# A decoder block on one core: float32 matmuls of attention and state space grouped into pairs and quarters, with four small edits beside it

## The chip, the core and the metric

The kernel runs on one core of a Trainium2 chip. A core has a matrix engine (TensorE, in the views PE, with PEld for its weight loads), a vector engine (VectorE, DVE), a scalar engine (ScalarE, ACT), a general engine (GpSimd, POOL) and a queue engine (SyncE, SP) that starts transfers. Each engine takes its instructions strictly in the order of the program; they meet at semaphores. The metric is the device time of one execution in microseconds (us), the median of the runs.

## The reference

One decoder layer on 256 tokens of width 1024. A normalised input is projected into q, k, v, u and a gate. Attention over eight heads and a state-space branch over u run side by side, are mixed by sigmoid gates, projected and added to the input; a squared-ReLU MLP and a last normalisation follow. All is float32.

```python
h = rms_norm(x, norm_mix_g)
q, k, v, u, g = split(h @ w_in)
q, k = rotary(q, pos), rotary(k, pos)
o_a = softmax(mask(q @ k.T * HEAD_DIM ** -0.5)) @ v          # 8 heads of 128, one block of 256 keys
# state space: a complex diagonal recurrence over 256 tokens, 32 groups of 64 states
xr0, xi0 = (cr + 1j * ci) * (u @ b)                          # per group
sr, si = scan(a, xr0, xi0)
y = sr @ c_re.T - si @ c_im.T + d_skip * u
val, gt = split(gelu(y) @ w_glu)
o_b = val * sigmoid(gt)
mixed = sigmoid(g_a) * o_a + sigmoid(g_b) * o_b
x = x + mixed @ w_out
x = x + square(relu(rms_norm(x, norm_mlp_g) @ w_up)) @ w_down
return rms_norm(x, norm_final_g)
```

## The kernel before

**Two kinds of matmul.** The large products (projections, GLU, output, MLP) split each float32 operand into a high and a low part and add three products of parts (`mm3`, `tok_mm`, `down`). ScalarE makes a weight tile's high part (`hi_`, line 83) and VectorE its low part (`lo_`, line 84), four tiles of each in turn, so a `hi_` cast waits until TensorE has left the tile four before it. The small products run on whole float32 operands, and each such instruction shows as two matmul records, a transpose as one: the scores `s` (`attn_head`, with two bf16 products that add the mask), the transposes `pt` of the probabilities and the outputs `o` (`attn_out`), the inputs `x` and outputs `y` of the state space (`ssm_quad`), the transposes `bt` of its input matrices (`prepare`), and `mt`, the transposes of the gated branch. `x` uses 64 rows of the array and `y` against `sr` and `si` 64 columns, so two of them run at a time; the others use the whole array.

**Attention** goes by four pairs of heads, S0 to S3 for scores and softmax, A0 to A3 for transposes, outputs and the multiply into `mixA`. The softmax of a head: two maxima on VectorE (`st`), two exponentials on ScalarE into `pr`, reciprocals on VectorE, two scalings of `pr` on ScalarE (lines 323, 324); then three transposes on TensorE, a copy `pts` on ScalarE, four matmuls.

**The state space** goes by four quads of state tiles: `tables(m)` makes cosines and sines of the phases (a high part by ScalarE, line 516, a low part by four VectorE instructions, line 520), `ssm_quad(m)` multiplies, scans and multiplies back. `prepare` builds the input matrices `Bs`, which GpSimd puts in place from `ab` (line 455).

**The order** of the work is written out by hand, in `ORDER`; Vn are the parts of v, Pn and Cn the preparation, Tn the tables, Kn the q and k of a pair, Gn its gate, Qn a quad, Bn the other gate, Xn the loads of ScalarE's function tables and Yn the gelu:

```python
ORDER = ("V0 V1 P0 T0 C0 Q0 T1 Q1 T2 K0 T3 X0 S0 G0 A0 G1 K1 K2 S1 Q2 A1 K3 G2 S2 A2 Q3 "
         "B0 G3 S3 X1 Y0 A3 B1")
```

A scheduler then lays each engine's instructions by due times of its own, with a lead for those under `high_priority` (the scores and outputs have `ATT_PRIO`), so the small matmuls come to lie within streams of large ones. `use_set` loads a table of functions (1.28 us) and holds each table's functions together: the exponentials of S3 must come before X1, and the gelus behind it.

Of the kernel before, what the change touches and what calls it, by code (L numbers as in the profile page):

```python
# [16 lines left out]
P = 128  # L17
# [31 lines left out]
def build(ctx, tc, dr, out):  # L49
# [45 lines left out]
    def behind(ins, others, reason="table set"):  # L95
        for o in others:
            tc.add_manual_dep(ins, o.name, mybir.DependencyInfo(
                mybir.DependencyClass.NoSync, mybir.DependencyReason.DATA), reason=reason)

    def use_set(func):  # L100
# [132 lines left out]
    for c in range(2):  # L233
        V.tensor_mul(u[:, 2 * c : 2 * c + 2], by_parity(u_acc[:, c]), rs_par)
    V.tensor_mul(rcos, cos_c, rs)
    V.tensor_mul(rsin, sin_c, rs)
    for q in range(4):
# [63 lines left out]

    scale = P ** -0.5
    mixA = p1.tile([P, KD, T], F32, name="mixA")

    def attn_head(q, k, j):
        s = att_bank("s").rearrange("p a b -> p (a b)")
        PE.matmul(s[:, 0:128], q[:, j, 0:128], k[:, j, 0:128], start=True, stop=False,
                  skip_group_check=True)
        PE.matmul(s[:, 0:128], ident_b, tri_b, start=False, stop=True, skip_group_check=True)
        PE.matmul(s[:, 128:384], q[:, j, 128:256], k[:, j, :], start=True, stop=False,  # L310
                  skip_group_check=True)
        PE.matmul(s[:, 256:384], ident_b, tri_b, start=False, stop=True, skip_group_check=True)
        st = p1.tile([P, 6], F32, tag="st", bufs=2, name="st")
        V.tensor_reduce(st[:, 0:1], s[:, 0:128], axis=mybir.AxisListType.X, op=ALU.max)
        V.tensor_reduce(st[:, 1:2], s[:, 128:384], axis=mybir.AxisListType.X, op=ALU.max)
        V.tensor_scalar(st[:, 0:2], st[:, 0:2], -scale, None, op0=ALU.mult)
        pr = p1.tile([P, 384], F32, tag="pr", bufs=2, name="pr")
        act(pr[:, 0:128], s[:, 0:128], AF.Exp, bias=st[:, 0:1], scale=scale,
                     accum_out=st[:, 2:3])
        act(pr[:, 128:384], s[:, 128:384], AF.Exp, bias=st[:, 1:2], scale=scale,  # L320
                     accum_out=st[:, 3:4])
        V.reciprocal(st[:, 4:6], st[:, 2:4])
        S.activation(pr[:, 0:128], pr[:, 0:128], AF.Copy, scale=st[:, 4:5])
        S.activation(pr[:, 128:384], pr[:, 128:384], AF.Copy, scale=st[:, 5:6])
        return pr

    def attn_pt(pr):
        pt = att_bank("pt").rearrange("p a b -> p (a b)")
        for i in range(3):
            PE.transpose(pt[:, i * P : (i + 1) * P], pr[:, i * P : (i + 1) * P], ident)  # L330
        pts = p1.tile([P, 384], F32, tag="pts", bufs=2, name="pts")
        S.copy(pts, pt[:, 0:384])
        return pts

    def attn_out(hp, prs, tha):
        pts = [attn_pt(x) for x in prs]
        o = att_bank("o")
        for j in range(2):
            hd = 2 * hp + j
            PE.matmul(o[:, j, :], v[:, 0, hd * P : (hd + 1) * P], pts[j][:, 0:256],  # L340
                      start=True, stop=False, skip_group_check=True)
            PE.matmul(o[:, j, 128:256], v[:, 1, hd * P : (hd + 1) * P], pts[j][:, 256:384],
                      start=False, stop=True, skip_group_check=True)
        V.scalar_tensor_tensor(mixA[:, 2 * hp : 2 * hp + 2, :], tha, 1.0, o,
                               op0=ALU.add, op1=ALU.mult)

# [12 lines left out]
    def prepare():  # L359
# [91 lines left out]

        def place(dst, k, src):
            for g in range(2):
                r = slice(64 * g, 64 * (g + 1))
                G.tensor_scalar(dst[r, :, k + 16 * g : k + 16 * (g + 1)], src[r], 1.0, None,
                                    op0=ALU.mult)

# [51 lines left out]
    def rot(name, bufs=1):  # L509
        return p1.tile([P, 4, P], F32, tag=name, bufs=bufs, name=name)  # L510

    def tables(m):
        hi, nlo = ssm[-2:]
        uhi, ang, cs, sn = rot("q", QK), rot("tha", 2), rot("cs", 4), rot("sn", 4)
# [15 lines left out]
    def ssm_quad(m):  # L530
# [31 lines left out]
        V.tensor_mul(w, d, cs)  # L562
        V.tensor_add(si, si, w)
        Wr, nWi, Dt = ssm[1:4]
        y = bank("y", 1, "y")
        for h in range(2):
            p = 2 * m + h
            PE.matmul(y[:, h, 0:P], Dt[:, p, :], U2[:, p, 1 : P + 1], start=(h == 0), stop=False,
                      skip_group_check=True)
# [75 lines left out]
    for q in range(4):  # L645
        acc = wide_banks(f"glu{q}") if q % 2 else [flat(mm_bank(f"glu{q}{h}")) for h in range(2)]
        for kk_ in range(2):
            wh, wl = w_unit(dr["w_glu"][2 * q + kk_], f"glu{q}{kk_}")
            for k2 in range(2):
                k, w = 2 * kk_ + k2, slice(k2 * 512, (k2 + 1) * 512)  # L650
                for hf in range(2):
                    tok_mm(acc[hf], wh[:, w], wl[:, w], yhl[0][:, 0:4], yhl[0][:, 4:8], k, hf,
                           k == 0, k == 3)
        tp = att_bank(f"mt{q}")
        for hf in range(2):
# [4 lines left out]
            V.scalar_tensor_tensor(tb, tb, 1.0, sg, op0=ALU.add, op1=ALU.mult)  # L660
# [222 lines left out]
```

## Time and profile before

| | |
|---|---|
| median of three runs | 397.01 us (397.0, 397.01, 402.53) |
| the profiled execution, its own time | 397.22 us |
| its span, first to last instruction | 395.4 us |
| TensorE busy, share of the span | 385.0 us, 97% |
| VectorE / ScalarE / GpSimd busy | 293.0 / 225.7 / 30.9 us |
| first matmul of the GLU / of the MLP | 165.67 / 213.61 us |
| first warm-up matmul / first matmul of u | 1.25 / 4.88 us |
| matmuls of u on 256 columns, start to start | 0.21 us until 10.4 us, 0.11 us from then on |
| matmuls on 512 columns, start to start (36.76, 36.99 us) | 0.23 us |
| one weight load of 128 columns | 0.188 us |

The busy share of TensorE counts records whose ends are modelled and overlap, so what a matmul really costs is read from one start to the next. An idle engine costs nothing unless TensorE waits for it, and TensorE's own idle time is in the brackets of its rows.

### The profile page before, as it was taken

The page shows a single profiled execution, that of the slowest core. Times are in us where ns is not written, and L with a number is a line of the kernel's source. Part 1 is how long each engine was busy: PE and PEld are TensorE (multiplying, and loading weights), DVE is VectorE, ACT ScalarE, POOL GpSimd, SP SyncE. Part 2 cuts the span into 40 slices and gives each one's busy share as a digit, 9 for nine tenths or more (in the row PEclk, how much of TensorE's full clock was granted, in tenths as well). Part 3 has the DMA queues.
Part 4 walks back from the last instruction along what each step waited for, and adds up shares of the span by engine and source line. Part 5 has one row for each costly group of instructions (what it writes and reads, how often), then busy time and mean ns, then how long its engine had stood idle before and what let it go on. Part 6 is the DMA issues. An engine that isn't in the chain of part 4 may idle for free.

```text
span 395.4 us, 6719 instructions
## 1 busy us (share of the span) xinstructions
PE 385.0 (97%) x2563; PEld 344.5 (87%) x2563; DVE 293.0 (74%) x521; ACT 225.7 (57%) x360; POOL 30.9 (8%) x39
## 2 busy tenths in 40 slices
PE   7999999999999999999999999999999999999993
PEld 4988898989899797888889999999999888888883
DVE  3999999999999997559748686676676444563434
ACT  5867886674466675955636755655556334354313
POOL 4242393000000000000000000000000000000000
PEclk9999999999999999999999999999999999999998
DMA  7995843344625354346486387556565566565202
GB/s 213 389 337 188 251 165 106 108 159 143 220 93 168 107 159 163 111 159 222 153 300 229 109 269 209 180 195 208 179 202 196 183 208 184 188 213 176 92 2 106
DMA packets 23199, 71.57 MB, mean 181 GB/s; under 512 B 2944, under 2 KB 5248, under 8 KB 23168
## 3 DMA queue, kind: packets, MB, share of 16 engines
q1 hardware_dynamic: 20144, 68.92, 53.1%
q10 hardware_dynamic: 3024, 2.23, 1.9%
q8 instruction: 20, 0.33, 0.3%
q14 instruction: 11, 0.09, 0.1%
HBM read 69.18 MB, written 1.05 MB: 178 GB/s over the span
## 4 chain that ended last, share of the span: by engine, by line
PE 86%; DVE 7%; DMA 2%; POOL 1%; issue 1%; ACT 1%; SPq 0%; ACTq 0%
PE up L88 7%; PE up L89 7%; PE up L90 7%; PE dn L736 6%; PE dn L734 6%; PE dn L735 5%; PE u_acc L181 3%; PE gb L269 2%; PE gb L267 2%; PE gb L268 2%; PE glu L269 2%; PE glu L267 2%; PE glu L268 2%; PE wo L268 2%; PE wo L269 2%; PE wo L267 2%
## 5 line engine op out<-in xcount | busy, mean ns | idle before, releaser
L89 PE MATMUL up<-x2l,hi_up 128*128 128x256 f32 x256 | 70.7, 277 | 0.0
L90 PE MATMUL up<-x2h,lo_up 128*128 128x256 f32 x256 | 70.5, 276 | 0.0
L88 PE MATMUL up<-x2h,hi_up 128*128 128x256 f32 x256 | 70.1, 276 | 0.0
L84 DVE TENSOR_TENSOR lo_dn<-raw_dn,hi_dn 128x1024 fp32r<-128x1024 f32 x32 | 39.2, 1225 | 40.4 <-ACT hi_dn L83 40.4
L83 ACT CAST hi_dn<-raw_dn 128x1024 fp32r<-128x1024 f32 x32 | 33.6, 1050 | 49.1 <-PE dn L736 24.6
L84 DVE TENSOR_TENSOR lo_up<-raw_up,hi_up 128x1024 fp32r<-128x1024 f32 x32 | 38.8, 1224 | 23.5 <-ACT hi_up L83 23.5
L83 ACT CAST hi_up<-raw_up 128x1024 fp32r<-128x1024 f32 x32 | 33.3, 1049 | 35.0 <-PE up L89 16.3
L89 PEld LDWEIGHTS up<-x2l,hi_up 128*128 128x128 f32 x256 | 48.1, 188 | 0.0
L90 PEld LDWEIGHTS up<-x2h,lo_up 128*128 128x128 f32 x256 | 48.1, 188 | 0.0
L88 PEld LDWEIGHTS up<-x2h,hi_up 128*128 128x128 f32 x256 | 47.8, 188 | 0.1
L735 PE MATMUL dn<-lo_dn,hh 128*128 128x512 f32 x96 | 37.4, 389 | 0.0
L736 PE MATMUL dn<-hi_dn,hl 128*128 128x512 f32 x96 | 37.4, 389 | 0.0
L734 PE MATMUL dn<-hi_dn,hh 128*128 128x512 f32 x96 | 37.4, 389 | 0.0
L736 PEld LDWEIGHTS dn<-hi_dn,hl 128*128 128x128 f32 x96 | 18.0, 188 | 3.7
L735 PEld LDWEIGHTS dn<-lo_dn,hh 128*128 128x128 f32 x96 | 18.0, 188 | 3.7
L734 PEld LDWEIGHTS dn<-hi_dn,hh 128*128 128x128 f32 x96 | 18.0, 188 | 3.7
L89 PE MATMUL g<-xgl,hi_g 128*128 128x256 f32 x64 | 18.5, 289 | 0.0
L88 PE MATMUL k<-xgh,hi_k 128*128 128x256 f32 x64 | 18.1, 282 | 0.0
L90 PE MATMUL q<-xgh,lo_q 128*128 128x256 f32 x64 | 18.1, 282 | 0.0
L90 PE MATMUL g<-xgh,lo_g 128*128 128x256 f32 x64 | 18.1, 282 | 0.0
L88 PE MATMUL g<-xgh,hi_g 128*128 128x256 f32 x64 | 18.0, 281 | 0.0
L89 PE MATMUL q<-xgl,hi_q 128*128 128x256 f32 x64 | 18.0, 281 | 0.0
(274 smaller groups left out, 1019.6 us busy)
## 6 DMA issues: line engine op xcount, KB each, us to landing
raw_up<-w_up SPq DMA_DIRECT2D x32, 512.0 KB, 4.3
raw_dn<-w_down SPq DMA_DIRECT2D x32, 512.0 KB, 4.3
raw_v<-w_in SPq DMA_DIRECT2D x8, 512.0 KB, 5.5
raw_q<-w_in SPq DMA_DIRECT2D x8, 512.0 KB, 3.3
raw_k<-w_in SPq DMA_DIRECT2D x8, 512.0 KB, 3.2
raw_g<-w_in SPq DMA_DIRECT2D x8, 512.0 KB, 3.8
raw_gb<-w_in SPq DMA_DIRECT2D x8, 512.0 KB, 4.3
raw_glu<-w_glu SPq DMA_DIRECT2D x8, 512.0 KB, 3.3
```

Source lines behind the costliest of these rows:

```text
L83: ins = S.copy(hi, x).ins
L84: V.tensor_sub(lo, x, hi.bitcast(F32))
L88: PE.matmul(o, wh, xh, start=first, stop=False, **kw)
L89: PE.matmul(o, wh, xl, start=False, stop=False, **kw)
L90: PE.matmul(o, wl, xh, start=False, stop=last, **kw)
L181: PE.matmul(u_acc[:, m // 2, m % 2, :], w[:, ws[m]], x[:, k, :], start=(k == 0 and i == 0 and m % 2 == 0), stop=(k == KD - 1 and i == 2), ...
L267: PE.matmul(acc, xh[:, k, rows], wh, start=first, stop=False)
L268: PE.matmul(acc, xh[:, k, rows], wl, start=False, stop=False)
L269: PE.matmul(acc, xl[:, k, rows], wh, start=False, stop=last)
L734: PE.matmul(acc, xh, wh[:, w], start=(k == lead), stop=False, skip_group_check=True)
L735: PE.matmul(acc, xh, wl[:, w], start=False, stop=False, skip_group_check=True)
L736: PE.matmul(acc, xl, wh[:, w], start=False, stop=(k == end), skip_group_check=True)
```

## The change

- **Grouping on TensorE.** A helper `after` adds a wait between two instructions. The six transposes of a pair wait until both heads' probabilities are scaled; its four output matmuls wait for the copies of both heads; a pair's scores wait until the pair before it has been multiplied into `mixA`; all ten instructions of a quad's `y` wait until `si` is complete; the four transposes `mt` of a group wait for both halves.
- **Phases.** The low part of the phases becomes four ScalarE instructions into a tile `ulo` and one VectorE addition.
- **Scores' scale.** The factor is put into the two rotation tables; the softmax loses one small VectorE instruction, and the maxima are negated where they are taken.
- **Input matrices.** The four placements into `Bs` go from GpSimd to ScalarE, with high priority.

```diff
+    def after(ins, others, reason):
+        for o in others:
+            tc.add_manual_dep(ins, o.name, mybir.DependencyInfo(
+                mybir.DependencyClass.Sync, mybir.DependencyReason.DATA), reason=reason)
...
-    V.tensor_mul(rcos, cos_c, rs)
-    V.tensor_mul(rsin, sin_c, rs)
+    V.scalar_tensor_tensor(rcos, cos_c, P ** -0.25, rs, op0=ALU.mult, op1=ALU.mult)
+    V.scalar_tensor_tensor(rsin, sin_c, P ** -0.25, rs, op0=ALU.mult, op1=ALU.mult)
...
+    left, scaled = [], []
     def attn_head(q, k, j):
-        PE.matmul(s[:, 0:128], q[:, j, 0:128], k[:, j, 0:128], start=True, stop=False,
-                  skip_group_check=True)
+        after(PE.matmul(s[:, 0:128], q[:, j, 0:128], k[:, j, 0:128], start=True, stop=False,
+                         skip_group_check=True).ins, left[-1:], "a pair's scores together")
...
-        V.tensor_reduce(st[:, 0:1], s[:, 0:128], axis=mybir.AxisListType.X, op=ALU.max)
-        V.tensor_reduce(st[:, 1:2], s[:, 128:384], axis=mybir.AxisListType.X, op=ALU.max)
-        V.tensor_scalar(st[:, 0:2], st[:, 0:2], -scale, None, op0=ALU.mult)
+        V.tensor_reduce(st[:, 0:1], s[:, 0:128], axis=mybir.AxisListType.X, op=ALU.max,
+                        negate=True)
...
-        S.activation(pr[:, 128:384], pr[:, 128:384], AF.Copy, scale=st[:, 5:6])
+        scaled.append(S.activation(pr[:, 128:384], pr[:, 128:384], AF.Copy, scale=st[:, 5:6]).ins)
...
-            PE.transpose(pt[:, i * P : (i + 1) * P], pr[:, i * P : (i + 1) * P], ident)
+            after(PE.transpose(pt[:, i * P : (i + 1) * P], pr[:, i * P : (i + 1) * P], ident).ins,
+                   [last], "a pair's transposes together")
...
     def attn_out(hp, prs, tha):
-        pts = [attn_pt(x) for x in prs]
+        last = scaled[2 * hp + 1]
+        pts = [attn_pt(x, last) for x in prs]
...
+            after(PE.matmul(o[:, j, :], v[:, 0, hd * P : (hd + 1) * P], pts[j][:, 0:256],
+                             start=True, stop=False, skip_group_check=True).ins,
+                   copied[-1:], "a pair's outputs together")
...
-        V.scalar_tensor_tensor(mixA[:, 2 * hp : 2 * hp + 2, :], tha, 1.0, o,
-                               op0=ALU.add, op1=ALU.mult)
+        left.append(V.scalar_tensor_tensor(mixA[:, 2 * hp : 2 * hp + 2, :], tha, 1.0, o,
+                                           op0=ALU.add, op1=ALU.mult).ins)
...
+                if urgent:
+                    with tc.high_priority(ATT_PRIO):
+                        S.copy(to, src[r])
+                else:
+                    G.tensor_scalar(to, src[r], 1.0, None, op0=ALU.mult)
...
-            place(Bs[c], 32, ab[c])
+            place(Bs[c], 32, ab[c], urgent=True)
...
+            S.activation(ulo[:, q, :], tpos, AF.Copy, scale=nlo[:, 4 * m + q : 4 * m + q + 1])
...
-        for q in range(4):
-            V.scalar_tensor_tensor(ang[:, q, :], tpos, nlo[:, 4 * m + q : 4 * m + q + 1],
-                                   ang[:, q, :], op0=ALU.mult, op1=ALU.add)
+        V.tensor_add(ang, ang, ulo)
...
-        V.tensor_add(si, si, w)
+        done = V.tensor_add(si, si, w).ins
...
-                    PE.matmul(y[64 * j : 64 * (j + 1), h, 0:P], w_[:, 4 * m + q, :], s_[:, q, :],
-                              start=False, stop=(i == 1), skip_group_check=True)
+                    after(PE.matmul(y[64 * j : 64 * (j + 1), h, 0:P], w_[:, 4 * m + q, :],
+                                     s_[:, q, :], start=False, stop=(i == 1),
+                                     skip_group_check=True).ins, [done], "y together")
...
+        for hf in range(2):
             for i in range(2):
-                PE.transpose(tp[:, i, hf * P : (hf + 1) * P], tb[:, i * P : (i + 1) * P], ident)
+                after(PE.transpose(tp[:, i, hf * P : (hf + 1) * P],
+                                    tbs[hf][:, i * P : (i + 1) * P], ident).ins,
+                       [merged], "a group's transposes together")
```

Three places show how the instructions move. The first is TensorE around the scores of the last pair, S3. Before, the second head's scores stand near the start of the last gate (`gb_2089` and `gb_2090`, made from `hi_` and `lo_` weights), whose remaining 44 matmuls follow it:

```order
L267 MATMUL gb_2090<-hi_gb_2093,xgh 128x512
L574 MATMUL y<-si,nWi 64x128 x4
L307 MATMUL s<-k,q 128x128
L309 LDWEIGHTS ident_b
L309 MATMUL s<-tri_b,ident_b 128x128
L310 MATMUL s<-k,q 128x256
L312 LDWEIGHTS ident_b
L312 MATMUL s<-tri_b,ident_b 128x128
L268 MATMUL gb_2090<-lo_gb_2094,xgh 128x512
L269 MATMUL gb_2090<-hi_gb_2093,xgl 128x512
```

Now, the same engine where the gate ends and the first head's scores begin:

```order
L273 MATMUL gb_2090<-lo_gb_2148,xgh 128x512
L274 MATMUL gb_2090<-hi_gb_2147,xgl 128x512
L313 MATMUL s<-k,q 128x128
L315 LDWEIGHTS ident_b
L315 MATMUL s<-tri_b,ident_b 128x128
L316 MATMUL s<-k,q 128x256
```

and four rows later, from the second head's scores on:

```order
L315 MATMUL s<-tri_b,ident_b 128x128
L316 MATMUL s<-k,q 128x256
L318 LDWEIGHTS ident_b
L318 MATMUL s<-tri_b,ident_b 128x128
L337 MATMUL pt<-cst,pr 128x128 x6
L272 MATMUL glu_2169<-hi_glu_2173,yhl 128x512
```

Both heads' scores have moved behind the last matmul of the gate, the pair's six transposes follow them directly, and the first matmul of the GLU follows those.

The second is ScalarE at the load of the gelu's table (`ACT_TABLE_LOAD`). Before, from the second head's exponentials of S3 to its scalings (`pr<-pr,st`); `yT` is the gelu:

```order
L107 ACTIVATE pr,st<-s,st 128x128
L107 ACTIVATE pr,st<-s,st 128x256
L101 ACT_TABLE_LOAD
L107 ACTIVATE yT<-yT 128x256 x2
L83 CAST hi_glu_2173<-raw_glu_2171 128x1024
L107 ACTIVATE yT<-yT 128x256
L585 COPY yT<-y 32x128
L323 ACTIVATE pr<-pr,st 128x128
L324 ACTIVATE pr<-pr,st 128x256
```

Now, from the second head's first exponential on (`thb` is the last gate's tanh):

```order
L112 ACTIVATE pr,st<-s,st 128x128
L330 ACTIVATE pr<-pr,st 128x128
L331 ACTIVATE pr<-pr,st 128x256
L112 ACTIVATE pr,st<-s,st 128x256
L106 ACT_TABLE_LOAD
L112 ACTIVATE yT<-yT 128x256 x4
L112 ACTIVATE thb_2087<-gb_2089,rs_half 128x256
L112 ACTIVATE thb_2088<-gb_2089,rs_half 128x256
L112 ACTIVATE thb_2087<-gb_2090,rs_half 128x256
L112 ACTIVATE thb_2088<-gb_2090,rs_half 128x256
L330 ACTIVATE pr<-pr,st 128x128
L331 ACTIVATE pr<-pr,st 128x256
```

The second head's scalings (the last two rows) have moved behind four gelus and four tanhs; before, three gelus, a cast and a copy stood between the table load and them.

The third is TensorE at the end of v. Before, the first transposes `bt` stood 56 rows further on, within q:

```order
L267 MATMUL v_384<-hi_v_442,xgh 128x512
L267 MATMUL v_385<-hi_v_442,xgh 128x512
L88 MATMUL q<-xgh,hi_q_872 128x256
L89 MATMUL q<-xgl,hi_q_872 128x256
L268 MATMUL v_384<-lo_v_443,xgh 128x512
```

Now:

```order
L272 MATMUL v_384<-hi_v_442,xgh 128x512
L272 MATMUL v_385<-hi_v_442,xgh 128x512
L487 MATMUL bt<-cst,Bs_610 128x128 x8
L88 MATMUL q<-xgh,hi_q_878 128x256
L89 MATMUL q<-xgl,hi_q_878 128x256
L273 MATMUL v_384<-lo_v_443,xgh 128x512
```

The first eight transposes `bt` have moved forward, into the last unit of v.

## Rows read from the trace of the kernel before

**Rows 1.** The page, busy time of each engine.
```profile
PE 385.0 (97%) x2563; PEld 344.5 (87%) x2563; DVE 293.0 (74%) x521; ACT 225.7 (57%) x360; POOL 30.9 (8%) x39
```

**Rows 2.** Timeline of PE: start, us, instruction, [idle before it and its releaser].
```profile
48.84 1.09 PE L471 MATMUL bt<-cst,Bs 128*128 128x128 f32 x8 [0.86 <-POOL Bs L455]
...
66.08 0.46 PE L307 MATMUL s<-k,q 128*128 128x128 f32 x2 [0.71 <-DVE k L299]
...
79.63 0.33 PE L330 MATMUL pt<-cst,pr 128*128 128x128 f32 x1 [0.49 <-ACT pr L323]
```

**Rows 3.** Timeline of PE around half of a quad's y.
```profile
89.34 0.28 PE L90 MATMUL k<-xgh,lo_k 128*128 128x256 f32 x1
89.55 0.66 PE L574 MATMUL y<-si,nWi 128*64 128x128 f32 x8
...
90.36 0.28 PE L89 MATMUL k<-xgl,hi_k 128*128 128x256 f32 x1
```

**Rows 4.** Timeline of PE where x and y alternate.
```profile
103.29 0.28 PE L90 MATMUL k<-xgh,lo_k 128*128 128x256 f32 x1
...
103.91 0.66 PE L574 MATMUL y<-si,nWi 128*64 128x128 f32 x8
104.50 1.16 PE L539 MATMUL x<-U,W 64*128 64x128 f32 x14
...
105.81 0.28 PE L89 MATMUL q<-xgl,hi_q 128*128 128x256 f32 x1
```

**Rows 5.** Timeline of PE around two whole-array matmuls of y.
```profile
92.83 0.28 PE L89 MATMUL q<-xgl,hi_q 128*128 128x256 f32 x1
92.95 0.60 PE L568 MATMUL y<-U,Dt 128*128 128x128 f32 x4
...
93.52 0.28 PE L88 MATMUL q<-xgh,hi_q 128*128 128x256 f32 x1
```

**Rows 6.** Timeline of DVE, one operation on 256 columns and one low part.
```profile
33.89 1.22 DVE L84 TENSOR_TENSOR lo_v<-raw_v,hi_v 128x1024 fp32r<-128x1024 f32 x1
...
37.01 0.41 DVE L235 TENSOR_TENSOR rcos<-cst,xg 128x256 f32<-128x256 f32 x1
```

**Rows 7.** Timeline of PE, the first use of that low part.
```profile
37.21 0.39 PE L268 MATMUL v<-lo_v,xgh 128*128 128x512 f32 x1
```

**Rows 8.** Timeline of PE, the last scores and the last transposes before the GLU.
```profile
154.87 0.22 PE L312 MATMUL s<-tri_b,ident_b 128*128 128x128 bf16 x1
...
165.42 0.49 PE L330 MATMUL pt<-cst,pr 128*128 128x128 f32 x3
```

**Rows 9.** Timeline of DVE between S3's heads.
```profile
154.32 1.20 DVE L84 TENSOR_TENSOR lo_gb<-raw_gb,hi_gb 128x1024 fp32r<-128x1024 f32 x1
...
155.66 0.40 DVE L315 TENSOR_REDUCE st<-s 128x1 f32<-128x256 f32 x1
```

**Rows 10.** Timeline of ACT from S3's exponentials on.
```profile
156.70 0.37 ACT L107 ACTIVATE pr<-s,st 128x128 f32<-128x128 f32 x1
...
157.63 1.28 ACT L101 ACT_TABLE_LOAD   x1
158.93 0.73 ACT L107 ACTIVATE yT<-yT 128x256 f32<-128x256 f32 x2
...
161.21 0.40 ACT L323 ACTIVATE pr<-pr,st 128x128 f32<-128x128 f32 x1
161.52 0.49 ACT L324 ACTIVATE pr<-pr,st 128x256 f32<-128x256 f32 x1
...
165.95 0.84 ACT L107 ACTIVATE thb<-gb,rs_half 128x256 f32<-128x256 f32 x2
```

**Rows 11.** Timeline of PE, four matmuls early in the kernel, and the last one.
```profile
9.77 0.92 PE L181 MATMUL u_acc<-xgl,hi_u 128*128 128x256 f32 x4
...
389.02 0.28 PE L736 MATMUL dnq<-hi_dn,hl 128*128 128x256 f32 x1
```

**Rows 12.** Windows after the last matmul: length, busy time per engine, granted clock.
```profile
392.70:395.40 2.70, 0.00 (x0) 0.00 (x0) 0.00 (x0) 0.00 (x0) 0.00 (x0) 0.50 0.52 194
```

More of the change, by code (lines that the diff above doesn't have):

```diff
@@ L300, in rope @@
         return o
-    scale = P ** -0.5
     mixA = p1.tile([P, KD, T], F32, name="mixA")
+    left, scaled = [], []
     def attn_head(q, k, j):
         s = att_bank("s").rearrange("p a b -> p (a b)")
-        PE.matmul(s[:, 0:128], q[:, j, 0:128], k[:, j, 0:128], start=True, stop=False,
-                  skip_group_check=True)
+        after(PE.matmul(s[:, 0:128], q[:, j, 0:128], k[:, j, 0:128], start=True, stop=False,
+                         skip_group_check=True).ins, left[-1:], "a pair's scores together")
         PE.matmul(s[:, 0:128], ident_b, tri_b, start=False, stop=True, skip_group_check=True)
@@ L313, in attn_head @@
         st = p1.tile([P, 6], F32, tag="st", bufs=2, name="st")
-        V.tensor_reduce(st[:, 0:1], s[:, 0:128], axis=mybir.AxisListType.X, op=ALU.max)
-        V.tensor_reduce(st[:, 1:2], s[:, 128:384], axis=mybir.AxisListType.X, op=ALU.max)
-        V.tensor_scalar(st[:, 0:2], st[:, 0:2], -scale, None, op0=ALU.mult)
+        V.tensor_reduce(st[:, 0:1], s[:, 0:128], axis=mybir.AxisListType.X, op=ALU.max,
+                        negate=True)
+        V.tensor_reduce(st[:, 1:2], s[:, 128:384], axis=mybir.AxisListType.X, op=ALU.max,
+                        negate=True)
         pr = p1.tile([P, 384], F32, tag="pr", bufs=2, name="pr")
-        act(pr[:, 0:128], s[:, 0:128], AF.Exp, bias=st[:, 0:1], scale=scale,
+        act(pr[:, 0:128], s[:, 0:128], AF.Exp, bias=st[:, 0:1],
                      accum_out=st[:, 2:3])
-        act(pr[:, 128:384], s[:, 128:384], AF.Exp, bias=st[:, 1:2], scale=scale,
+        act(pr[:, 128:384], s[:, 128:384], AF.Exp, bias=st[:, 1:2],
                      accum_out=st[:, 3:4])
@@ L323, in attn_head, with attn_pt @@
         S.activation(pr[:, 0:128], pr[:, 0:128], AF.Copy, scale=st[:, 4:5])
-        S.activation(pr[:, 128:384], pr[:, 128:384], AF.Copy, scale=st[:, 5:6])
+        scaled.append(S.activation(pr[:, 128:384], pr[:, 128:384], AF.Copy, scale=st[:, 5:6]).ins)
         return pr
-    def attn_pt(pr):
+    def attn_pt(pr, last):
         pt = att_bank("pt").rearrange("p a b -> p (a b)")
         for i in range(3):
-            PE.transpose(pt[:, i * P : (i + 1) * P], pr[:, i * P : (i + 1) * P], ident)
+            after(PE.transpose(pt[:, i * P : (i + 1) * P], pr[:, i * P : (i + 1) * P], ident).ins,
+                   [last], "a pair's transposes together")
         pts = p1.tile([P, 384], F32, tag="pts", bufs=2, name="pts")
-        S.copy(pts, pt[:, 0:384])
+        copied.append(S.copy(pts, pt[:, 0:384]).ins)
         return pts
+    copied = []
     def attn_out(hp, prs, tha):
-        pts = [attn_pt(x) for x in prs]
+        last = scaled[2 * hp + 1]
+        pts = [attn_pt(x, last) for x in prs]
         o = att_bank("o")
@@ L339, in attn_out @@
             hd = 2 * hp + j
-            PE.matmul(o[:, j, :], v[:, 0, hd * P : (hd + 1) * P], pts[j][:, 0:256],
-                      start=True, stop=False, skip_group_check=True)
+            after(PE.matmul(o[:, j, :], v[:, 0, hd * P : (hd + 1) * P], pts[j][:, 0:256],
+                             start=True, stop=False, skip_group_check=True).ins,
+                   copied[-1:], "a pair's outputs together")
             PE.matmul(o[:, j, 128:256], v[:, 1, hd * P : (hd + 1) * P], pts[j][:, 256:384],
                       start=False, stop=True, skip_group_check=True)
-        V.scalar_tensor_tensor(mixA[:, 2 * hp : 2 * hp + 2, :], tha, 1.0, o,
-                               op0=ALU.add, op1=ALU.mult)
+        left.append(V.scalar_tensor_tensor(mixA[:, 2 * hp : 2 * hp + 2, :], tha, 1.0, o,
+                                           op0=ALU.add, op1=ALU.mult).ins)
     def gate(first, dst):
@@ L450, in cmul, with place @@
             (V.tensor_sub if neg_i else V.tensor_add)(o_i, o_i, w)
-        def place(dst, k, src):
+        def place(dst, k, src, urgent=False):
             for g in range(2):
                 r = slice(64 * g, 64 * (g + 1))
-                G.tensor_scalar(dst[r, :, k + 16 * g : k + 16 * (g + 1)], src[r], 1.0, None,
-                                    op0=ALU.mult)
+                to = dst[r, :, k + 16 * g : k + 16 * (g + 1)]
+                if urgent:
[3 more added lines that the diff above has]
+                    G.tensor_scalar(to, src[r], 1.0, None, op0=ALU.mult)
         Bs = [p1.tile([P, ST, 64], F32, tag=f"y{c}", name=f"Bs{c}") for c in range(2)]
@@ L513, in tables @@
         hi, nlo = ssm[-2:]
+        ulo = rot("ulo")
         uhi, ang, cs, sn = rot("q", QK), rot("tha", 2), rot("cs", 4), rot("sn", 4)
@@ L567, in ssm_quad @@
             p = 2 * m + h
-            PE.matmul(y[:, h, 0:P], Dt[:, p, :], U2[:, p, 1 : P + 1], start=(h == 0), stop=False,
-                      skip_group_check=True)
+            after(PE.matmul(y[:, h, 0:P], Dt[:, p, :], U2[:, p, 1 : P + 1], start=(h == 0),
+                             stop=False, skip_group_check=True).ins, [done], "y together")
         for i, (w_, s_) in enumerate(((Wr, sr), (nWi, si))):
@@ L654, in build @@
         tp = att_bank(f"mt{q}")
+        tbs = []
         for hf in range(2):
@@ L659, in build @@
             tb = thb[q][:, hf, :]
-            V.scalar_tensor_tensor(tb, tb, 1.0, sg, op0=ALU.add, op1=ALU.mult)
+            merged = V.scalar_tensor_tensor(tb, tb, 1.0, sg, op0=ALU.add, op1=ALU.mult).ins
+            tbs.append(tb)
+        for hf in range(2):
             for i in range(2):
-                PE.transpose(tp[:, i, hf * P : (hf + 1) * P], tb[:, i * P : (i + 1) * P], ident)
+                after(PE.transpose(tp[:, i, hf * P : (hf + 1) * P],
+                                    tbs[hf][:, i * P : (i + 1) * P], ident).ins,
+                       [merged], "a group's transposes together")
         two = slice(2 * q, 2 * q + 2)
```

## The prediction

> **What bounds the kernel now.** I read the page's first part, then TensorE's waits, then its timeline wherever a small matmul stands. TensorE is busy 97% of the span [rows 1], and behind the first microseconds, while inputs arrive, it stands idle for another engine at three places only, 0.86, 0.71 and 0.49 us [rows 2]. So nearly every microsecond by which TensorE's queue grows or shrinks goes into the end, and what the other engines gain or lose counts only where TensorE waits for it. Start to start is the measure: an ordinary matmul on 256 columns takes 0.11 us, a small record on 128 columns 0.11 us too [rows 5], and one on 512 columns 0.23 us.
>
> **Grouping.** Eight records of y that use half the array stand between two ordinary matmuls; from 89.34 to the second ordinary matmul after them, at 90.36, go 1.02 us, of which 0.23 belong to the two ordinary ones and 0.44 to four pairs of records [rows 3]. The visit cost 0.35 us beyond its work. Where x, y and x alternate, 2.52 us go for 1.55 us of work, 0.97 us for three visits [rows 4]. A visit with the whole array costs 0.02 us: 0.69 us for 0.67 [rows 5]. Counted in the order of the instructions, half-array visits go from 17 to 10 and whole-array groups from 29 to 11. That is 7 x 0.33 + 18 x 0.02 = **2.7 us less**; bounds 0 (joined matmuls may still be switched one by one) and 3.5.
>
> One page speaks otherwise. The Trainium skill, "TensorE: Matmul & The Clock Gate", section "The mechanism" (Part 3), says that a weight load overlaps a running matmul only where its row group differs. By it each whole-array visit would cost its weight load, and the gain would be larger; the 0.02 us of rows 5 speak against it, and I keep to the rows.
>
> **The three stalls.** The 0.86 us before `bt` ended with GpSimd's placement. ScalarE now places as soon as `ab` is there. `bt` is moved forward to about 40.8 us; counting VectorE's new order, the first `ab` is done near 36, and ScalarE's queue reaches the copies near 38.5, so it is free with some 2 us to spare. The first scores stand 37 ordinary matmuls later than they did, 4 us, and their stall was 0.71 us; the first transposes also come 4 us later in their stream. All three go: **2.1 us less**; bounds 0 and 2.6 (start to start).
>
> **Phases, scale, v.** The four small VectorE instructions saved, the twelve fewer phase instructions and the 16 more on ScalarE lie beside TensorE's stream and cost nothing by themselves, as long as the `hi_` and `lo_` tiles come in time. They are closest in v. Before, a low part started at 33.89 and was ready at 35.11 [rows 6], 2.1 us ahead of its first use at 37.21 [rows 7]. In the new order VectorE has ahead of it five more operations of 0.33 us (0.41 long, next start after 0.33) [rows 6], two on 512 columns (0.6, an estimate from the same row), eight tiny ones of 0.09, less 0.8 for the shorter phases: 2.75 us. Ready at 37.9, wanted at 37.4 since a second high product now goes first: **0.5 us more**; bounds 0 and 1.2.
>
> **The added waits.** Pairs 0 to 2 have 12 us or more of large matmuls between their scores and their transposes, where the chain between needs about 7 (below); the quads' y stand as late. I cost them at nothing; an uncovered one would show as the stalls of rows 2, some 0.7 us each.
>
> Pair 3 has no cover. Its scores now stand behind the last matmul of the last gate, since they wait until pair 2 is multiplied out and the gate went ahead. Directly behind them stand the pair's six transposes, which wait for both heads' scaled probabilities, and behind these the GLU, which wants the gelus that ScalarE does behind the same exponentials. TensorE keeps its order, as the third stall shows, where q's matmuls with all their operands stood behind one transpose [rows 2]. Before, 44 gate matmuls filled the time between the last scores at 154.87 and the last transposes at 165.42 [rows 8]. Now TensorE is idle for that chain.
>
> Its length, counted from the gate's last matmul: scores of one head 0.75 us (records of 0.11 and 0.21, two small ones of 0.05), of both 1.5. The first head's maxima are done at 1.5, its exponentials at 2.4. VectorE does a low part of 1.15 between the heads and then two maxima, at most 0.4 each [rows 9]: second head at 3.3. ScalarE then has the second head's exponentials, 0.93 (156.70 to 157.63); the first head's scalings, 0.7; the table load, 1.3; four gelus, 1.3 (0.73 for two with their overlap); four tanhs, 1.5; the second head's scalings, 0.7 [rows 10]. 3.3 + 6.4 = 9.7, and 0.1 to TensorE: 9.8, less the 1.5 in which TensorE still does scores, is **8.2 us more** (0.1 rounded off). Bounds: 6.9, the time that the old chain took from the end of the last scores (155.1) to the end of the second scaling (162.0) [rows 8, 10], and 9.
>
> **The clock.** Early in the kernel matmuls on 256 columns start 0.21 us apart (four in 0.92) [rows 11], at the lower level, 1.2 GHz, and later 0.11. The last matmul starts at 389.02 [rows 11], and the granted clock from 392.7 on is 0.50 [rows 12]. So an idle stretch of 8 us ends at the lower level, and the next matmuls run at half rate until it rises. How long, no row shows for this place. At the start the matmuls of u were slow from 4.88 to 10.4 us, with gaps, which cost about 2.5 us; counted from the first warm-up matmul it was 9 us, which at 0.43 for 0.23 us would lose 4.2. I take the nearer one and less, since the stream here has no gaps: **2.2 us more**; bounds 0 and 4.2.
>
> **Sum.** Against the profiled execution's 397.2 us: 397.2 - 2.7 - 2.1 + 0.5 + 8.2 + 2.2 = 403.3. The median of the runs lies 0.2 below that execution, so 403.1 us, 1.5% slower.
>
> **Rivals.**
> *The clock stays low long* (slower by more than 2%). If the lower level lasts as long after the idle stretch as from the first warm-up matmul, 9 us, it costs 4.2 instead of 2.2: 405.1. It decides from about 8.5 us on. For it: the start. Against it: gaps there, none here. Another uncovered wait of 0.7 us comes out at the same. Chance 0.21.
> *A short chain and no fall of the clock.* 6.9 instead of 8.2 and 0 instead of 2.2: 399.6. The fall at the end of the kernel speaks against it. Chance 0.09.
> *The grouping pays and nothing is idle*, because the matmuls behind a waiting transpose go on: 397.0 - 2.7 - 2.1 + 0.5 = 392.7. The 79.63 us row speaks against it [rows 2]. Chance 0.04.
> *The change does not do what it says*: x and y joined in the queue still cost a switch for each part, so the 2.7 come back, with the idle stretch as forecast: 405.8. Against it: three visits in rows 4 cost three times one. Chance 0.05.
> *Whole-array groups were dear*, 0.19 us for each of 18: 3.4 instead of 0.4, 400.1. Rows 5 speak against it; it is what the page's rule would give. Chance 0.03.
>
> **How the numbers follow.** The forecast, 401.0 to 404.9, has 0.58. About 2%, 7.9 us, is what a measurement of this kernel can tell from no change, so the bounds are 389.1 and 404.9. Faster: only the lower part of the third rival, 0.01. Slower: the first rival's upper half, 0.13, the fourth, 0.04, and 0.05 of the forecast's own upper edge: 0.22. The rest, 0.77, is within 2%. The range leaves out the third rival, the lower half of the second and what lies over 406: 399.6 to 406.0.
>
> **What would show it.** An idle stretch of TensorE of about 8 us that ends with the transposes `pt` of the last pair, released by ScalarE's scaling, between the last gate and the GLU; a granted clock of 0.50 behind it, matmuls on 512 columns 0.43 us apart; no stall before `bt`, the first `s` or the first `pt`; y of a quad in one piece of 20 records with one switch. I am wrong if the last pair's scores run while the gate still has matmuls, if ScalarE reaches the second scaling within 4 us, or if some other added wait stops TensorE for microseconds.

## The result and the profile after

The changed kernel takes 407.9 us, the median of six runs (406.6 to 409.5), where the kernel before took 397.0 beside it: ratio 1.027, 95% interval 1.024 to 1.030. It is slower, as forecast, but by 2.7% and not by 1.5%, and the time lies above the range. Its profiled execution took 409.2 us, with a span of 407.3; it is the one that is taken apart below, 1.3 us above the median.

The first part of its page, and the clock's line of the second, 40 slices of 10.2 us each (beside [rows 1]):

```profile
PE 385.8 (95%) x2563; PEld 346.1 (85%) x2563; DVE 288.8 (71%) x501; ACT 231.5 (57%) x380; POOL 27.7 (7%) x35
...
PEclk9999999999999989779999999999999999999998
```

TensorE's busy time is nearly what it was (385.0 us before), though part of it now runs at a lower clock. The span grew by 11.9 us, and what was added lies mostly between 145 and 179 us, as idle time and as a lower clock. TensorE's timeline at the three places of [rows 2]:

```profile
41.34 1.04 PE L487 MATMUL bt<-cst,Bs 128*128 128x128 f32 x8
...
69.05 0.49 PE L313 MATMUL s<-k,q 128*128 128x128 f32 x2
...
84.72 0.82 PE L337 MATMUL pt<-cst,pr 128*128 128x128 f32 x6
```

No bracket is left there: the three stalls are gone. A quad's y stands in one piece (beside [rows 3 to 5]):

```profile
91.03 0.28 PE L89 MATMUL q<-xgl,hi_q 128*128 128x256 f32 x1
91.14 0.60 PE L584 MATMUL y<-U,Dt 128*128 128x128 f32 x4
91.68 0.66 PE L590 MATMUL y<-sr,Wr 128*64 128x128 f32 x8
92.17 0.61 PE L590 MATMUL y<-si,nWi 128*64 128x128 f32 x8
...
92.93 0.28 PE L88 MATMUL q<-xgh,hi_q 128*128 128x256 f32 x1
```

From 91.03 to 92.93 are 1.90 us, 0.38 beyond the work (two ordinary matmuls, four whole records, eight pairs of half records): one switch for the whole quad, where half a quad cost 0.35. The kernel then waits in new places. TensorE's waits, in us in total, times, longest:

```profile
PE pt L337 <- ACT pr L331: 8.0, 1, 8.0
PE gb L272 <- DVE tha L361: 2.4, 1, 2.4
...
PE gb L272 <- DVE q L302: 0.5, 1, 0.5
PE o L351 <- ACT pts L340: 0.5, 1, 0.5
PE up L89 <- DVE x2l L719: 0.4, 1, 0.4
PE v L273 <- DVE lo_v L84: 0.4, 1, 0.4
```

The first is the idle stretch that was forecast. TensorE and then ScalarE around it (beside [rows 8, 10]):

```profile
166.24 0.22 PE L318 MATMUL s<-tri_b,ident_b 128*128 128x128 bf16 x1
174.45 1.54 PE L337 MATMUL pt<-cst,pr 128*128 128x128 f32 x6 [8.00 <-ACT pr L331]
...
177.50 0.63 PE L272 MATMUL glu<-hi_glu,yhl 128*128 128x512 f32 x1
177.93 0.63 PE L273 MATMUL glu<-lo_glu,yhl 128*128 128x512 f32 x1
```

```profile
169.64 1.28 ACT L106 ACT_TABLE_LOAD   x1
170.93 1.33 ACT L112 ACTIVATE yT<-yT 128x256 f32<-128x256 f32 x4
172.17 1.54 ACT L112 ACTIVATE thb<-gb,rs_half 128x256 f32<-128x256 f32 x4
...
173.89 0.51 ACT L331 ACTIVATE pr<-pr,st 128x256 f32<-128x256 f32 x1
```

Between the scores and the second head's scaling ScalarE has the table load, four gelus and four tanhs, in the order that the prediction counted. Behind the stretch the GLU's matmuls start 0.43 us apart. The second wait is one that the prediction does not have. The last gate's first matmul wants an accumulator bank, and VectorE's multiply of the other gate (`tha`, L361), which by the profile empties that bank, is third in its queue when TensorE has finished that gate. TensorE's and VectorE's timelines:

```profile
145.67 0.28 PE L90 MATMUL g<-xgh,lo_g 128*128 128x256 f32 x1
148.35 0.77 PE L272 MATMUL gb<-hi_gb,xgh 128*128 128x512 f32 x1 [2.40 <-DVE tha L361]
148.91 0.63 PE L273 MATMUL gb<-lo_gb,xgh 128*128 128x512 f32 x1
```

```profile
145.79 1.21 DVE L84 TENSOR_TENSOR lo_gb<-raw_gb,hi_gb 128x1024 fp32r<-128x1024 f32 x1
146.91 0.69 DVE L578 TENSOR_TENSOR sw__1856<-rd,cs 128x512 f32<-128x512 f32 x1
147.51 0.69 DVE L361 TENSOR_TENSOR tha<-g,xg 128x512 f32<-128x512 f32 x1
```

ScalarE's second tanh of the gate ahead, which empties another bank, ends 0.2 us behind this multiply, at 148.40. Two things have moved there. The other gate's matmuls `g` now run in one piece, from 140.32 us on; before, pair 2's transposes and outputs, pair 3's first scores and parts of y lay between them, and the last gate began at 152.41. And ScalarE's four tanhs, which read the gate ahead, start at 147.59, behind both of pair 2's scalings, and not at 143.65. TensorE's and ScalarE's timelines before:

```profile
152.41 0.39 PE L267 MATMUL gb<-hi_gb,xgh 128*128 128x512 f32 x1
...
143.65 0.82 ACT L107 ACTIVATE thb<-gb,rs_half 128x256 f32<-128x256 f32 x2
```

and ScalarE's now:

```profile
147.59 1.54 ACT L112 ACTIVATE thb<-gb,rs_half 128x256 f32<-128x256 f32 x4
```

So TensorE comes to the last gate 6.5 us sooner, and the banks come free later; run 8 tells the two apart.

Windows behind both waits (length, busy time of PE, PEld, DVE, ACT, POOL, granted clock, DMA share, GB/s; beside [rows 12]):

```profile
148.30:151.60 3.30, 3.25 (x8) 2.62 (x9) 2.03 (x3) 1.34 (x4) 0.00 (x0) 0.50 0.78 235
...
174.40:178.90 4.50, 4.45 (x14) 3.77 (x15) 1.52 (x4) 2.20 (x6) 0.00 (x0) 0.50 0.00 0
178.90:184.00 5.10, 5.10 (x26) 4.35 (x25) 1.15 (x2) 1.04 (x1) 0.00 (x0) 1.00 0.00 0
```

So the clock fell twice. Start to start, the sum for the last matmul (389.02 before, 400.95 after, 11.9 us later) is:

| step | forecast, us | measured, us |
|---|---|---|
| grouping | -2.7 | -2.5 |
| three stalls gone | -2.1 | -2.6 |
| v's late low part | +0.5 | +0.5 |
| idle stretch before the last `pt` | +8.2 | +8.2 |
| half clock behind it | +2.2 | +2.1 |
| last gate waits for its bank | 0 | +2.6 |
| half clock behind that | 0 | +1.6 |
| `o`, `gb` behind it, `g`, `up` wait | 0 | +2.1 |
| u's phase at the start (first matmul of v at 20.45, before at 19.95) | 0 | +0.5 |
| not assigned | 0 | -0.6 |

Grouping and stalls are the time beyond the work around all groups of small matmuls, 10.7 us before and 5.6 after when the new waits and the half-rate matmuls are taken out; 2.6 of the 5.1 belong to the three stalls (1.03, 0.88 and 0.66 with their switches).

### The profile page after: what moved, and what is told of

Read it like the earlier page. It is cut to its first block, busy times and chain, and to the rows that moved or that the text cites. A ratio compares the mean times of both kernels' runs of the same rounds, so it can differ in the third digit from the quotient of the medians.

```text
span 407.3 us, 6710 instructions
## 1 busy us (share of the span) xinstructions
PE 385.8 (95%) x2563; PEld 346.1 (85%) x2563; DVE 288.8 (71%) x501; ACT 231.5 (57%) x380; POOL 27.7 (7%) x35
## 4 chain that ended last, share of the span: by engine, by line
PE 74%; DVE 12%; DMA 6%; issue 3%; ACT 2%; POOL 1%; SPq 0%; DVEq 0%; ACTq 0%
PE up L89 7%; PE up L90 7%; PE up L88 7%; PE dn L758 5%; PE dn L757 5%; PE dn L756 5%; DMA x2t<-x 2%; PE glu L272 2%; PE glu L273 2%; PE k L88 2%; PE glu L274 2%; PE q L88 2%; PE q L90 2%; PE q L89 2%; PE k L89 2%
## 5 line engine op out<-in xcount | busy, mean ns | idle before, releaser
L88 PE MATMUL q<-xgh,hi_q 128*128 128x256 f32 x64 | 18.0, 281 | 0.0
```

The lines of the kernel that those rows point to most:

```text
L88: PE.matmul(o, wh, xh, start=first, stop=False, **kw)
```

## The experiments

Theory A: the waits added in attention leave pair 3's chain uncovered, and that is the main loss. Rival B: the edits on the other engines moved the order and make the loss. Theory C: the wait at 145.9 us is the accumulator bank. All runs compute the whole reference. "Before" is the kernel before, run beside them: 396.9 us in the first eight, 397.1 to 397.2 in the last four.

**1. No attention waits.**

```diff
-...ins, left[-1:], "a pair's scores together")
+...ins, [], "a pair's scores together")
...
-                   [last], "a pair's transposes together")
+                   [], "a pair's transposes together")
...
-                   copied[-1:], "a pair's outputs together")
+                   [], "a pair's outputs together")
```

> Leaves out the added waits of attention alone (scores behind the previous pair, transposes behind the pair's last scaling, outputs behind the last copy); the waits of y and of the GLU transposes and all the small edits stay. Now 50 large matmuls stand between pair 3's first scores and its last transposes. Theory A, the uncovered chain of pair 3 is what these waits made: the 8.2 us idle stretch and the 2.4 us of slow matmuls behind it go, some 1.0 us of switches come back: 407.9 - 8.2 - 2.4 + 1.0 = 398.3 us; if the 2.4 us wait for the gate's bank and its slow matmuls (1.9 us) belong to the same waits, 394. Theory B, the loss comes from the edits on the other engines (ScalarE's phases and placement, the scale): 404 us or more.

Measured: 396.1 us, ratio to before 0.998 (0.995 to 1.000). Both losses are gone, the granted clock reads 1.00 until the last matmuls, and what TensorE waits for behind u is short:

```profile
PE glu L272 <- DVE sg L676: 1.1, 1, 1.1
PE v L273 <- DVE lo_v L84: 0.5, 1, 0.5
```

The second head's scores of pair 3 start at 152.0 us and the last transposes at 161.8, with gate matmuls and y between them. A holds. The bank's wait belongs to the same waits: it is gone from the trace too, and 396.1 is nearer to 394 than to 398.3 once the new stall at 180 us (1.1 us idle) is counted. B falls: all the edits are still in this kernel.

**2. The waits without the edits.** Phases, scale and placement are written as before (their three hunks of the diff reversed); `after(...)` stays everywhere.

> All the added waits, without the three small edits (phases, scale and placement as in the kernel before). Theory A: the idle stretch of 8 us before the last pair's transposes and the low clock behind it stay: 405 to 409 us. Theory B, the edits beside it make the loss: about 394 us. The stall of 0.9 us before bt should be back and v's wait of 0.5 us gone, in both.

Measured: 408.1 us, ratio 1.027 (1.022 to 1.032), the same as with the edits. Its largest waits of TensorE:

```profile
PE pt L336 <- ACT pr L330: 8.7, 2, 8.3
PE gb L272 <- ACT thb L112: 1.3, 1, 1.3
```

The gate's bank is awaited here too, held, as the profile has it, by ScalarE's tanhs of the gate before and not by VectorE's multiply, and the stall before `bt` (0.5 us) is back. B is refuted from the other side.

**3. The last gate in banks of its own.**

```diff
+        if late:                                   # late = (first == 36)
+            b = ps.tile([P, 2, 2, T], F32, tag="x", name="gbx")
+            acc = [flat(b[:, h]) for h in range(2)]
...
```

> The last gate matmul group (B1) accumulates in the two banks of x, which no one reads any more, instead of the ring of three; nothing else is changed. Theory C, the 2.4 us for which TensorE waits at 145.9 is the bank that VectorE's gate multiply and ScalarE's tanhs hold, and the slow matmuls behind it are its clock: 2.4 to 4.3 us less, 403.6 to 405.5 us, no granted clock of 0.5 near 148. Rival: the wait only moves to the pair's transposes or scores a few us later: 407 to 409 us.

Measured: 403.6 us, 4.3 us less than the changed kernel. The window over the place of the old stall:

```profile
145.00:152.00 7.00, 7.00 (x33) 5.76 (x33) 5.99 (x10) 6.01 (x12) 0.00 (x0) 1.00 0.71 224
```

TensorE works through and the clock stays at 1.0: C holds, with the price of its upper end. TensorE's wait for the last scaling is still 8.0 us; it only starts 4.7 us earlier.

**4. The idle stretch filled** with matmuls that nobody reads (`behind` is the kernel's helper that orders two instructions of one engine without a wait).

```diff
+                    hold = flat(ps.tile([P, 2, 2, T], F32, tag="x", name="hold")[:, 0])
...
+                    for _ in range(30):
+                        behind(PE.matmul(hold, xgh[:, 0, 0:P], xf[:, 0:512], start=True,
+                                         stop=True, skip_group_check=True).ins, lasts[-1:], "hold")
```

> 30 matmuls on 512 columns, whose result nobody reads, behind the last pair's scores (6.9 us of the 8.2 us idle stretch); all work of the kernel is kept. Theory A: TensorE's clock stays at 1.0 there and the slow matmuls behind the stretch go: 2.4 us less, 405.5 us, and the transposes start when they did. Rival, the matmuls behind the stretch are slow for want of operands, not of clock: 408 us. If the chain on ScalarE were shorter than 6.9 us, the time would grow.

Measured: 406.1 us, 1.8 less where 2.4 were forecast. TensorE's timeline, and the window over the matmuls behind the gate's stall:

```profile
165.16 7.09 PE L643 MATMUL hold<-xgh 128*128 128x512 f32 x30
173.35 0.87 PE L338 MATMUL pt<-cst,pr 128*128 128x128 f32 x6 [1.10 <-ACT pr L332]
...
174.29 0.39 PE L273 MATMUL glu<-lo_glu,yhl 128*128 128x512 f32 x1
174.53 0.39 PE L272 MATMUL glu<-hi_glu,yhl 128*128 128x512 f32 x1
174.76 0.40 PE L273 MATMUL glu<-lo_glu,yhl 128*128 128x512 f32 x1
```

```profile
148.60:152.00 3.40, 3.33 (x15) 2.77 (x16) 2.05 (x3) 1.36 (x4) 0.00 (x0) 1.00 0.80 261
```

From the end of the scores to the transposes it is 8.2 us as before, and the GLU's matmuls behind them start 0.23 us apart instead of 0.43. The slow matmuls were the clock's, since the filling changes nothing in the chain of their operands. In this profile the gate's stall was there in full, 2.4 us, and the clock did not fall behind it.

**5. Only y's waits and the edits.** Run 1 with the GLU's transposes written as before the change (each pair right behind its own `tb`, no `after`).

> The run without attention waits, and the GLU's transposes ungrouped again too; what stays of the grouping is y of a quad in one piece, and all the small edits stay. In the run without attention waits TensorE stood 1.2 us at 180 us between grouped GLU transposes and the next GLU group, whose bank VectorE still read. Theory: that stall is the grouping's, it goes, 396.1 - 1.2 = 394.9 us, 0.5% below the kernel before. Rival: the stall is VectorE's load and comes back elsewhere: 396 us.

Measured: 401.8 us, ratio 1.011 (1.008 to 1.013): neither. The GLU's stall is still there (its wait for `sg`, 0.8 us where run 1 had 1.1), so the grouping of its transposes had not made it, and a larger one has appeared at the MLP's start. TensorE, and VectorE's operation that the chain to it goes back to:

```profile
213.32 0.50 PE L88 MATMUL up<-x2h,hi_up 128*128 128x256 f32 x2 [0.40 <-ACT x2h L713]
217.25 0.38 PE L89 MATMUL up<-x2l,hi_up 128*128 128x256 f32 x1 [3.43 <-DVE x2l L714]
```

```profile
210.92 1.29 DVE L707 SCALAR_TENSOR_TENSOR x2t<-wo,x2t 128x512 f32<-128x512 f32 x2 [4.92 <-DMA x2t<-x]
```

Before, and in run 1, the first transposes of the residual (`xt`) stand 2.5 to 3 us ahead of the last `wo` matmul; here they stand behind it, with the `up` matmuls directly after, so nothing covers the chain from `x2t` over `xt` to `x2h` and `x2l`. The clock fell there too (0.50 from 218.2 to 221.6 us).

**6. The edits alone**: run 5 without y's waits.

> No grouping waits at all, all the small edits. The instructions' order has one half-array visit and four whole-array groups more than with y grouped: 0.33 + 4 x 0.02 = 0.4 us more than that run, 395.3 us. Rival, y's wait costs TensorE more than it saves: 394.5 us or less. Against the kernel before: the three stalls (2.4 us from start to start) less v's 0.5 us: 397.0 - 1.9 = 395.1 us.

Measured: 395.0 us, ratio 0.995 (0.993 to 0.997). This is the fastest version, 0.5% below the kernel before, and the time is what was forecast for it, the stalls less v's low part. The terms fit less well: its trace has no wait in v, while v's first matmul starts 0.7 us later than before, so the agreement is in part luck. That it lies below run 5 is run 5's order at the MLP, and tells nothing of y's price; run 1, with y grouped and no such stall, is 1.2 us above it, about its GLU stall. Both runs with y grouped have that stall and this one has not; whether y's waits make it was not followed.

**7. Scores free, 8. transposes free.** In each, one of the waits of run 1's diff is left out.

> Only the wait of the scores for the previous pair is left out of the changed kernel. In the order, the last pair's first head then has its scores 24 large matmuls ahead of the transposes, the second head only 4. Theory A1, either wait alone is enough to leave the chain uncovered, because the second head's scores still wait for a bank that the previous pair's output holds, and the transposes for the second head: idle 6 to 8 us remains, 405 to 408 us. Rival A2, the scores' wait alone is the cause: 397 to 399 us.

> Only the wait of the transposes for the pair's second scaling is left out of the changed kernel. The last pair's scores still stand behind the last gate matmul and the six transposes directly behind them. Theory A1: idle 7 to 8 us remains, ended by the first head's scaling or by the second's, 406 to 409 us. Rival A3, the transposes' wait alone is the cause: 397 to 399 us.

Measured: 407.3 us and 404.7 us. TensorE's timeline before the GLU, first of run 7, then of run 8:

```profile
171.47 1.54 PE L337 MATMUL pt<-cst,pr 128*128 128x128 f32 x6 [6.85 <-ACT pr L331]
```

```profile
165.21 0.83 PE L337 MATMUL pt<-cst,pr 128*128 128x128 f32 x3 [2.36 <-ACT pr L330]
170.82 1.09 PE L337 MATMUL pt<-cst,pr 128*128 128x128 f32 x3 [4.78 <-ACT pr L330]
```

A1 holds: either wait alone leaves about 7 us. In run 7 the second head's scores stand at 162.65, in run 8 both heads' at 161.0, and only four gate matmuls or none follow. Run 8 came out 1.3 us under its range, and what is gone is the wait before the last gate: its 1.3 us wait for a bank stands ahead of the first of the two gates `gb`, at 126 us. TensorE and ScalarE at the last one:

```profile
146.29 0.40 PE L272 MATMUL gb<-hi_gb,xgh 128*128 128x512 f32 x1
```

```profile
144.50 1.56 ACT L112 ACTIVATE thb<-gb,rs_half 128x256 f32<-128x256 f32 x4
```

TensorE comes to it as early as in the changed kernel, with `g` in one piece, and finds a bank free, since the tanhs start 3.1 us sooner, ahead of pair 2's scalings; the multiply `tha` is as late as it was (148.21). In run 7 the 2.4 us are there in full. So the wait of the transposes makes the last gate's wait, and TensorE's early arrival alone does not.

**9. Three quarters, 10. half of the last gate behind the scores**, with all grouping kept.

```diff
+        for mm in (...the three matmuls of tok_mm...):
+            behind(mm.ins, hold, "gate behind the last scores")
...
+                           lasts[-1:] if first == 36 and kk_ >= 1 else ())   # 10: kk_ >= 2
```

> The changed kernel with all its grouping waits, and one more order on TensorE: the last three quarters of the last gate (36 matmuls on 512 columns, 8.2 us) stand behind the last pair's scores, no longer ahead of them. Theory A: they cover the chain from the scores to the transposes, so the 8.2 us idle stretch and the 2.4 us of slow matmuls go; ahead of the scores stay stalls of 2 to 3 us while pair 2's scalings, its output and its merge are awaited: 394 to 397 us. Grouping then gives what it was costed at. Rival, the idle stretch is bound to the GLU (gelus behind the exponentials), and only moves behind the gate: 401 us or more.

> The same with only the last half of that gate (24 matmuls, 5.5 us) behind the scores. Theory A: 8.2 - 5.5 = 2.7 us of the idle stretch stay ahead of the transposes, the stalls ahead of the scores are shorter by up to 2 us: 395 to 399 us. Rival as in the other run: 401 us or more.

Measured: 399.1 us, ratio 1.004 (1.002 to 1.006), and 401.6, ratio 1.010 (1.007 to 1.013). The two largest of run 9's waits behind the start:

```profile
PE gb L274 <- DVE tha L366: 2.4, 1, 2.4
...
PE s L317 <- DVE mixA L361: 0.8, 1, 0.8
```

The 8 us wait is gone from run 9, and the rival with it: the chain needs cover, not an earlier end of the gelus. Both runs lie 2 us or more above what I expected, because I let the gate's bank wait shrink, and it stayed whole with half clock behind it (0.50 from 149.7 to 153.1 us in run 9). By its time alone run 10 would fit the rival (401 us or more); in its trace the wait before the last transposes is 1.0 us, with 0.4 us before the GLU, so the rival falls there too.

**11. Run 5 with x's load ahead of the fourth `up` weight on SyncE's queue, 12. run 9 with run 3's banks and this load.**

```diff
+        if name.startswith("up"):
+            ups.append(ld)
+            if len(ups) > 3:
+                behind(ld.ins, xload, "x ahead of the later weights")
```

> The run with y's waits and the edits (401.8 us), with one more order on SyncE's queue: the load of x for the residual stands in the queue where it stood in the changed kernel, ahead of the fourth of the up weights, not one place behind it. Theory D: in that run x landed at 210.8 instead of 205.4 us, VectorE's residual waited for it 4.9 us, and the up matmuls behind it 3.4 us, with 1.7 us of slow matmuls; these go: 401.8 - 3.6 - 1.7 = 396.5 us. The stall of 1.0 us behind the first GLU transposes, which was there without their grouping too, stays. Rival, the up stall comes from the later transposes of x alone: 400 us or more.

> All grouping waits of the changed kernel, with the last three quarters of the last gate behind the last scores, that gate's sums in the banks of x, and the load of x at its place in the queue. Theory C: the wait for the gate's bank (2.4 us) and the slow matmuls behind it (1.9) go from the 399.1 us of the run without the two last changes. What stands in its place is the chain of pair 2: its scalings end near 147.7, y's last operand at 149.9, so some 1.7 us are lost ahead of its transposes and of y: 396.5 us. If these stalls lie beside others, 394.8; if the clock falls there again, 398.5.

Measured: 401.6 us and 402.6 us, ratio 1.011 and 1.012. In run 11 x comes earlier (VectorE's residual at 207.85 instead of 210.92), and nothing is won: the wait before the `up` matmuls breaks into several (0.6, 0.9 and 0.3 us, where run 5 had 0.4 and 3.4), and the clock falls again (0.57 on average from 216 to 220 us). First run 11's VectorE, then run 12's waits of TensorE:

```profile
207.85 1.29 DVE L713 SCALAR_TENSOR_TENSOR x2t<-wo,x2t 128x512 f32<-128x512 f32 x2 [2.44 <-DMA x2t<-x]
```

```profile
PE up L95 <- DVE x2l L735: 2.0, 1, 2.0
PE v L281 <- DVE lo_v L90: 1.8, 1, 1.8
```

Theory D, x's late load as the cause, falls. Its rival, that the place of the transposes `xt` alone makes the stall, fits both, since run 12's order has them late too. It also fits the versions without the stall: VectorE waits for x there as well (4.1 us before, 2.7 in run 1, 4.7 in the changed kernel), but `xt` stands ahead of the last `wo` matmul. No run moved `xt` alone. The gate's wait is gone from run 12 as C says: from q's first matmul to the GLU's go 121.6 us (43.98 to 165.53) instead of run 9's 126.0 (42.58 to 168.56). Then 5.5 us are lost between the GLU's first matmul and the last one (228.7 us, in run 9 223.2), at the MLP's start for the most part. And q starts 1.4 us later, behind the 1.8 us at v's low part with half clock after it (0.50 from 40 to 43 us).

## Why the prediction was right and wrong

**Right, mechanism and size.** The grouping gave 2.5 us for 2.7: a visit of y to half the array costs what [rows 3] showed, however many records it holds. The Trainium skill, "TensorE: Matmul & The Clock Gate", section "The mechanism" (Part 3), says that a weight load overlaps running matmuls only where the row group differs; the same section also names a background weight buffer into which a load is pulled ahead. By the first, eighteen fewer whole-array visits at the 0.188 us of a weight load would have gained 3.0 us more than the 0.02 us a visit of [rows 5], as an estimate; the measured 2.5 us has no room for that, so the rows were the better guide. No run shows whether such a buffer is the reason. The three stalls (2.6 us, the upper bound, for 2.1), v's 0.5 us, the idle stretch before the last `pt` (8.2) and the half clock behind it (2.1 for 2.2) came out as summed. For v that holds in this execution: its wait grows where u's phase ends sooner, from none in run 6 (v's first matmul at 20.62 us) to 1.7 us in run 7 (at 19.35). Runs 1, 2 and 4 show that the stretch is made by the waits and the slow matmuls by the clock. The size of the last term was in part luck. It was set below 2.5 us by judgement, from u's slow matmuls at the start; there the lower level was read off the distance of the matmuls, while the granted clock of that trace reads 1.00 until 10.4 us.

**Wrong: the step "The added waits … I cost them at nothing".** It looked only at whether large matmuls lie between a pair's scores and its transposes, and there the cover held: no transposes of pairs 0 to 2 wait. It did not ask what stands behind those waits on VectorE and ScalarE. With pair 2's heads together, its scalings end at 147.7 us, and around them low parts, y's rotations, the tanhs of one gate and the multiply of the other come late and empty the accumulator banks late. TensorE, which has the last gate next, waits 2.6 us for a bank, and the clock falls: 4.2 us, which run 3 takes away (4.3). Run 1 shows that the attention waits bring it about, run 8 that it is the wait of the transposes, without which the tanhs go ahead of the scalings and the last gate waits for nothing. Run 2, where a tanh (`thb`) is awaited and not `tha`, shows that which operation holds the bank depends on the order. The other small waits, 2.1 us together, are of the same step, and run 1 has none of them; in the prediction's words they would "show as the stalls of rows 2, some 0.7 us each", and three of that size did (0.67, 0.69, 0.61 from start to start) with a smaller one, though the sum held none. The step is 6.3 us wrong in all.

**What the rivals were worth.** Nearest by its time was "The change does not do what it says" (405.8), but y's one switch for a whole quad refutes it. "The clock stays low long" came near the time (405.1), for the wrong reason: behind the idle stretch the clock cost 2.1 us. It named a further uncovered wait of 0.7 us as its equal, where there was one of 2.6 with a clock fall of its own.

**Open.** Which of VectorE's operations ahead of `tha` matters to the bank's wait was not tried, nor why the scheduler put the tanhs behind the scalings. Why the order puts `xt` late in runs 5, 11 and 12 is the planner's, and was not followed. No run shows all the grouping with every chain covered, so whether its 2.5 us can be had in whole is not settled.

## What to carry to other kernels

A wait that holds small matmuls together delays all of them to the last operand, so count, from the last score to the first transpose, how much other work still stands behind the wait in TensorE's queue; either of two such waits was enough to lose 7 us for a gain of 2.5. Then follow what the waiting group holds up on the other engines, down to who empties the accumulator banks. Where a planner sets the order, an edit in one stage can move a chain in another: read the whole order again, since here taking back the GLU's grouping, a harmless-looking edit, cost 5.7 us (run 5 against run 1), most of it at the MLP.

## What the runs showed of the hardware

A stall of 2.4 us before the last gate was followed by a granted clock of 0.50 for about 3.4 us in the profiles of the changed kernel (from 148.2 us), of run 9 (from 149.7) and of run 10 (from 149.4), but not in those of runs 4 and 7, with a stall of the same length, nor behind the stalls of 1.3 us in run 2 (at the last gate) and run 8 (at 126 us). At v's low part a stall of 1.75 us was followed by such a fall in run 12 (0.50 from about 40 to 43.4 us) and by none in run 7. In runs 9, 10 and 12 the first matmuls behind the stall still ran at the full rate. So in these traces the stall of 2.4 us costs 2.6 or about 4.2 us. Behind the 8 us stretch TensorE started again at 174.45 and ran at the lower level until 178.92, in run 3 from 169.7 to 173.8: 2.1 us lost, half of what the start of the kernel had suggested as the upper bound.
